# State-space tables of a hybrid backbone on one core: X stored in one transfer, loads for two steps, a second lag buffer, lags read one yield earlier

## Chip, cores and metric

The kernel runs on 1 core of one Trainium2 chip. The metric is device time in microseconds (us) of one execution; the time before is the median of three runs. The core has a matrix engine (TensorE, PE in the profile, with its weight loads as PEld), three elementwise engines (VectorE or DVE, ScalarE or ACT, GpSimd or POOL) and SyncE (SP), which in this kernel issues every transfer to the 16 DMA engines. Everything is float32; the big products are split into three products of a high and a low half.

## What is computed

The reference is a backbone of two layers over 1024 latent tokens and 256 context tokens of width 1024. Layer 0 mixes tokens by differential attention, layer 1 by a bidirectional diagonal complex state-space layer (S5); each mixer is followed by a dense MLP with squared ReLU. The change concerns constants of the S5 layer alone. For each of 2 directions and 64 groups of 16 channels, S5 runs a recurrence over 64 complex states:

```python
lam_bar = jnp.exp(lam * dt)
b_bar = ((lam_bar - 1.0) / lam)[..., None] * b_mat
...
bu = jnp.einsum('gpc,btgc->btgp', b_bar, uc.astype(jnp.complex64))
a_cum, hs = lax.associative_scan(_linear_combine, (a, bu), axis=1)
hs = hs + a_cum * h[:, None]
y = jnp.real(jnp.einsum('gcp,btgp->btgc', c_mat, hs))
```

The kernel doesn't step token by token. It takes 8 tokens at once: powers of lam_bar times b_bar bring 8 tokens' inputs into the states (the matrix X, here transposed from XT), powers of lam_bar times c_mat bring a state to 8 tokens' outputs (W), and within the 8 tokens the inputs reach the outputs through products of both, one small matrix for each distance in time (the lag products, 16 x 16 for each group and lag). All three depend on parameters only, so they are made as tables before the S5 layer runs.

## The kernel before

The program is written with a tile framework: instructions are given in program order, and a scheduler with a model of their times puts each engine's instructions in an order of its own and adds the waits. Every engine, SyncE with its transfers among them, then runs its own list strictly in order, so an instruction that waits holds all behind it on that engine.

**Where the tables are made.** The tables are built beside the down projection of layer 0's MLP, `mlp0_down` (L1596). That stage has 53 blocks. A block runs two of 112 steps q, each of 5 token groups x 3 matmuls (`mm3`, L132 to L134: high x high, high x low, low x high) of 512 columns. For every q, `mlp0_load` (L1572) brings an activation block and a weight block from HBM (transfers U<-Aa, U<-Ta and U<-in_mlp_w) three blocks ahead, and `mlp0_prep` (L1590) splits both into halves: ScalarE copies the high half (L137), VectorE subtracts it from the source (L138). At the end of every run of 16 steps an accumulator is evacuated to the sums FD by ScalarE (L1618) or added to them by VectorE (L1620). After each block's matmuls, `self.step(2)` (L1654) takes two steps of background work, a list of generators; each goes to its next `yield`. The first generator is `s5_phases` (two yields), the second `s5_tables` (L1125). At block 40, what is left of them is drained, and the normalisation of finished token tiles begins (`m0_tile`, L1688): tile 1 loads its residual into `fv(48)` to `fv(52)`.

**The generator `s5_tables`.** It has 32 table steps, in the order `todo`: for each of four groups c, four indices q of direction 0 and four of direction 1; an index covers four (direction, group) positions x. Loop iteration i does, in program order:

- `load(i + 1)` (L1146): three transfers of 64 to 68 KB into slot (i+1) mod 4 of `ins`: the powers tp (from tpd), C (tc, from tcd) and B (tb, from tbd).
- `matrices(i)` (L1151): six VectorE operations, L1153 to L1155 for W and L1160 to L1162 for XT, and one transfer of W to the table `recd`. W and XT have three buffers each.
- a yield, then `products(i - 2)` (L1164): four transposes of XT on TensorE into the PSUM bank `acc` (L1168), one ScalarE copy of the bank to a buffer Xs of 4 x 128 columns (L1169), and two transfers of it to `recd`. There a row has 4 x 192 columns: 128 columns, then the first 64 of them once more. Then four matmuls of tb with W into the bank `acc2` (L1174; the profile counts eight records), one ScalarE copy of their 128 columns to half `q % 2` of the only lag buffer `Ks` (L1176), and after each odd q four transfers of Ks to the table `kd`. Then a yield. Xs has two buffers, `acc` and `acc2` one each.
- after each 8 steps, `lags(c)` (L1182): three transfers bring lag products from kd (kv is a view of it) into k and f0; VectorE adds the two directions' lag 0 (L1188) and the skip term (L1190); one transfer stores k to `ktd`; a yield; four transfers copy ktd with repeated lags to `lagd`; a yield.

The yields of both generators add up to 76, or 38 blocks.

**Where things lie.** U is a tile of 62 KB per partition, of which the tables use `u(0)` to `u(30)` and the projection's loads the part from `u(30)` to `u(61)`. FD (`self.F`, 56 KB) holds the sums in 0 to 40; `s5_phases` works in 40 to 49.5. Offsets count in KB. `recd` and `lagd` are read by the S5 layer (`s5`, L1782), which follows the stage.

Of the kernel before, what the change touches and what calls it, by code (L numbers as in the profile page):

```python
# [9 lines left out]
AF = mybir.ActivationFunctionType  # L10
# [37 lines left out]
def shaped(ap, dims):  # L48
    if len(dims) == 1:
        return ap  # L50
    names = "abcd"[: len(dims)]
    kw = {n: d for n, d in zip(names[1:], dims[1:])}
    return ap.rearrange(f"p ({' '.join(names)}) -> p {' '.join(names)}", **kw)


def bcast(ap, axis, n):
    dims = [list(d) for d in ap.ap]
    dims.insert(axis, [0, n])
    return bass.AP(ap.tensor, ap.offset, dims)
# [11 lines left out]
class Prog:  # L71
# [414 lines left out]
    def lam_setup(self):  # L486
# [5 lines left out]
        st = self.lamc = self.cst.tile([128, 12], F32, name="lamc")  # L492
        nc.vector.tensor_reduce(st[:, 0:2], pr, AX.X, ALU.add)
        nc.scalar.activation(st[:, 2:4], st[:, 0:2], AF.Exp)
# [630 lines left out]
    def s5_tables(self, o, acc, acc2):  # L1125


        nc, I = self.nc, self.I
        v, tt = nc.vector, nc.vector.tensor_tensor
        u = lambda off, *dims: self.view(self.U, off, dims)  # L1130
        ins = [(u(x, 4, 34), u(x + 0.5625, 4, 32), u(x + 1.0625, 4, 32)) for x in (o + 1.5625 * i for i in range(4))]
        Wr = [u(o + 6.25 + 2.25 * i, 4, 9, 16) for i in range(3)]
        t, XTr = u(o + 13, 576), [u(o + 15.25 + 2 * i, 4, 8, 16) for i in range(3)]
        Xr = [u(o + 21.25 + 2 * i, 4, 128) for i in range(2)]
        t4, t2, Ks = shaped(t, (4, 9, 16)), shaped(t[:, 0:512], (4, 8, 16)), u(o + 25.25, 2, 128)
        k, f0, mask, dc = u(o + 26.25, 2, 15, 16), u(o + 28.25, 2, 16), u(o + 28.5, 16), u(o + 28.75, 8)
        self.dma(mask, I["dmask"])
        d0, d1 = u(o + 29, 128)[0:8], u(o + 29.5, 128)[0:8]
        self.dma(d0, I["s5_d"][0].rearrange("(y x) -> y x", x=128))
        v.tensor_copy(d1.rearrange("y (e c j) -> y e j c", c=16, j=4), d0.rearrange("y (e j c) -> y e j c", c=16, j=4))  # L1140
        nc.tensor.transpose(acc[:, 0:8], d1, self.ident[0:8, 0:8])
        nc.scalar.activation(dc, acc[:, 0:8], AF.Copy)
        kv = self.kd.rearrange("d (y e) c j n -> d (e c j) y n", e=2)
        todo = [16 * d + 4 * c + r for c in range(4) for d in range(2) for r in range(4)]

        def load(i):  # L1146
            x0 = 4 * todo[i]
            for dst, src in zip(ins[i % 4], (self.tpd, self.tcd, self.tbd)):
                self.dma(dst, src[:, x0 : x0 + 4])

        def matrices(i):  # L1151
            (tp, tc_, tb_), W, XT, q = ins[i % 4], Wr[i % 3], XTr[i % 3], todo[i]
            tt(W, bcast(tc_[:, :, 0:16], 2, 9), bcast(tp[:, :, 0:9], 3, 16), ALU.mult)  # L1153
            tt(t4, bcast(tc_[:, :, 16:32], 2, 9), bcast(tp[:, :, 9:18], 3, 16), ALU.mult)
            tt(W, W, t4, ALU.add)  # L1155
            d = q // 16
            w0 = 1 - d
            self.dma(shaped(self.recd[q % 16][:, 1536 + 512 * d : 2048 + 512 * d], (4, 128)),
                     W[:, :, w0 : w0 + 8].rearrange("p x i c -> p x (i c)"))
            tt(XT, bcast(tb_[:, :, 0:16], 2, 8), bcast(tp[:, :, 18:26], 3, 16), ALU.mult)  # L1160
            tt(t2, bcast(tb_[:, :, 16:32], 2, 8), bcast(tp[:, :, 26:34], 3, 16), ALU.mult)
            tt(XT, XT, t2, ALU.add)  # L1162

        def products(i):  # L1164
            tb_, W, XT, Xs, q = ins[i % 4][2], Wr[i % 3], XTr[i % 3], Xr[i % 2], todo[i]
            d = q // 16
            for j in range(4):
                nc.tensor.transpose(acc[:, 128 * j : 128 * j + 128], XT[:, j].rearrange("p s c -> p (s c)"), self.ident)  # L1168
            nc.scalar.activation(Xs.rearrange("p x n -> p (x n)"), acc, AF.Copy)  # L1169
            X = shaped(self.recd[q % 16][:, 768 * d : 768 * d + 768], (4, 192))  # L1170
            self.dma(X[:, :, 0:128], Xs)
            self.dma(X[:, :, 128:192], Xs[:, :, 0:64])
            for j in range(4):
                nc.tensor.matmul(acc2[32 * j : 32 * j + 32, 0:128], tb_[:, j],  # L1174
                                 W[:, j, d : d + 8].rearrange("p i c -> p (i c)"), start=True, stop=True)
            nc.scalar.activation(Ks[:, q % 2], acc2[:, 0:128], AF.Copy)  # L1176
            if q % 2:
                for j in range(4):
                    dst = self.kd[d, q % 16 - 1 : q % 16 + 1, :, j].rearrange("h c n -> c h n")
                    self.dma(dst, Ks[32 * j : 32 * j + 16])  # L1180

        def lags(c):  # L1182
            ys = slice(2 * c, 2 * c + 2)
            kk = k.rearrange("p y m c -> p y (m c)")
            self.dma(kk[:, :, 0:128], kv[1][:, ys])
            self.dma(kk[:, :, 128:240], kv[0][:, ys, 16:128])
            self.dma(f0, kv[0][:, ys, 0:16])
            tt(k[:, :, 7], k[:, :, 7], f0, ALU.add)  # L1188
            for y in range(2):
                v.scalar_tensor_tensor(k[:, y, 7], mask, dc[:, 2 * c + y : 2 * c + y + 1], k[:, y, 7], ALU.mult, ALU.add)  # L1190
            self.dma(self.ktd.rearrange("(y e) c j n -> (e c j) y n", e=2)[:, ys], kk)
            yield
            for h in range(4 * c, 4 * c + 4):
                src = self.ktd[h]
                src = bass.AP(src.tensor, src.offset + 16 * 7, [[240, 64], [-16, 8], [1, 128]])
                self.dma(self.lagd[h].rearrange("(s c) (j n) -> (c j) s n", s=8, j=4), src)
            yield

        load(0)
        for i in range(34):  # L1200
            if i < 31:
                load(i + 1)
            if i < 32:
                matrices(i)
            yield
            if i > 1:
                products(i - 2)
                yield
            if i > 1 and (i - 1) % 8 == 0:
                yield from lags((i - 1) // 8 - 1)  # L1210
# [571 lines left out]
    def s5(self):  # L1782
# [54 lines left out]
        def inputs(n, d):  # L1837
            X = slots[n % 2][0] if n else shaped(x_first, (2, 4, 192))
            cols = slice(0, 160) if d == 0 else slice(32, 192)
            for j in range(2):  # L1840
                b = xbank(n, d, j)
                for i in range(4):
                    o = 512 * (i // 2) + 160 * (i % 2)
                    mm(b[:, o : o + 160], X[:, d, i, 64 * j : 64 * j + 128], U[:, 4 * n + i, cols], start=True, stop=True)  # L1844

# [26 lines left out]
        def outputs(n):  # L1872
            X, W1, T, W2, _ = slots[n % 2]
            for i in range(4):
                o = self.bank(6 + n % 2)[:, 128 * i : 128 * i + 128]
                mm(o, U[:, 4 * n + i, 32:160], T[:, i], start=True, stop=False)  # L1876
                for d in range(2):
                    for j, W in enumerate((W1, W2)):
                        mm(o, cs[d][n % 2][j][:, i], W[:, d, i], start=False, stop=d == 1 and j == 1)  # L1879
# [588 lines left out]
```

## Time and profile before

| what | us |
|---|---|
| median of three runs (2878.24 to 2882.3) | 2880.2 |
| the profiled execution | 2870.1 |
| its span, first to last instruction | 2868.3 |
| TensorE busy | 2730.3 |
| VectorE busy | 2016.2 |
| ScalarE busy | 1363.1 |
| GpSimd busy | 1021.6 |
| first load of the tables issued | 1400.7 |
| last lag transfer issued | 1711.8 |

The profile is one execution, on the chip, taken by the hardware profiler. An instruction stands there with its start, its duration, its engine, its line, the tiles it writes and reads (out<-in) and, in brackets, how long its engine had been idle before it and what ended that. "A <- B" in the list of waits reads: A waited for B; then the total, the number of times and the longest. SPq is SyncE's queue of transfers, L80 the helper that issues all of them, so they are told apart by tiles. The granted clock (PEclk) is TensorE's clock as a share of full speed. Busy matmuls overlap: a matmul of 512 columns lasts some 0.39 us, and the next starts before it ends.

### The profile page before, as it was taken

How to read it: one execution, taken by the hardware profiler on the slowest of the kernel's cores; microseconds unless marked ns; L12 is line 12 of the kernel's file. 1: busy time of each engine (PE TensorE's matmuls, PEld its weight loads, DVE VectorE, ACT ScalarE, POOL GpSimd, SP SyncE). 2: the span in 40 equal slices, each digit the busy share in tenths (PEclk: the TensorE clock that was granted, in tenths of full speed). 3: DMA queues.
4: the chain of work that ended last, by engine and by line, in shares of the span. 5: the costliest groups of instructions: out<-in, count | busy, mean ns of one | idle time of the engine just before them, and what ended most of it. 6: DMA issues, size and time to landing. Idle time of an engine off the chain costs nothing. (4 is left out here: it accounts for less than half of the span.)

```text
span 2868.3 us, 43597 instructions
## 1 busy us (share of the span) xinstructions
PE 2730.3 (95%) x15225; PEld 2281.8 (80%) x15225; DVE 2016.2 (70%) x2968; ACT 1363.1 (48%) x2551; POOL 1021.6 (36%) x899
## 2 busy tenths in 40 slices
PE   7999999999899999999999999789999999999999
PEld 4688888888777887878877778688788778878887
DVE  5456788888863666666788767799533597668456
ACT  3425556555554743333444335477444633344443
POOL 2314666676663600000010013588121243336314
PEclk9999999999999999999999999899999999999999
DMA  9955555555826468885899887479743144466544
GB/s 299 309 169 175 153 173 175 177 175 169 255 83 190 120 212 306 296 305 192 272 294 299 260 244 242 156 232 295 253 140 110 59 159 164 158 235 235 165 131 141
DMA packets 447786, 586.33 MB, mean 204 GB/s; under 512 B 60494, under 2 KB 293196, under 8 KB 444364
## 3 DMA queue, kind: packets, MB, share of 16 engines
q1 hardware_dynamic: 447564, 583.53, 63.9%
q8 instruction: 120, 1.97, 0.3%
q14 instruction: 102, 0.84, 0.1%
HBM read 396.38 MB, written 182.82 MB: 202 GB/s over the span
## 5 line engine op out<-in xcount | busy, mean ns | idle before, releaser
L132 PE MATMUL PS<-H 128*128 128x512 f32 x1056 | 416.0, 395 | 8.6 <-DVE FD L1620 5.7
L134 PE MATMUL PS<-H 128*128 128x512 f32 x1056 | 413.8, 393 | 1.6 <-DVE H L2139 1.3
L133 PE MATMUL PS<-H 128*128 128x512 f32 x1056 | 414.8, 393 | 0.0
L132 PE MATMUL PS<-H,R 128*128 128x512 f32 (+1 forms) x828 | 307.5, 374 | 3.6 <-ACT R L137 1.6
L133 PE MATMUL PS<-H,R 128*128 128x512 f32 (+1 forms) x828 | 298.2, 360 | 1.4 <-POOL H L138 1.4
L134 PE MATMUL PS<-H,R 128*128 128x512 f32 (+1 forms) x828 | 297.6, 360 | 0.0
L132 PEld LDWEIGHTS PS<-H 128*128 128x128 f32 x1056 | 199.4, 189 | 55.0 <-issue 6.4
L134 PEld LDWEIGHTS PS<-H 128*128 128x128 f32 x1056 | 199.6, 189 | 45.3 <-DVE H L2139 1.7
L133 PEld LDWEIGHTS PS<-H 128*128 128x128 f32 x1056 | 199.7, 189 | 41.5 <-issue 1.0
L545 ACT ACTIVATE F<-F,stat 128x1280 f32<-128x1280 f32 x128 | 174.4, 1363 | 106.2 <-DVE F L535 105.9
L132 PE MATMUL PS<-R,H 128*128 128x512 f32 x536 | 213.6, 401 | 1.4 <-ACT R L137 1.4
L137 ACT ACTIVATE R<-W 128x512 fp32r<-128x512 f32 (+1 forms) x186 | 130.8, 712 | 172.3 <-PE PS L133 99.2
L133 PE MATMUL PS<-R,H 128*128 128x512 f32 x536 | 210.9, 394 | 0.0
L134 PE MATMUL PS<-R,H 128*128 128x512 f32 x536 | 209.3, 394 | 1.7 <-DVE H L138 1.7
L137 ACT ACTIVATE H<-U 128x640 fp32r<-128x640 f32 x216 | 132.9, 678 | 150.9 <-PE PS L133 104.5
L138 DVE TENSOR_TENSOR H<-W,H 128x512 fp32r<-128x512 f32 (+1 forms) x137 | 124.2, 917 | 103.8 <-ACT H L137 103.1
L138 DVE TENSOR_TENSOR H<-U,H 128x640 fp32r<-128x640 f32 x216 | 165.9, 805 | 39.7 <-ACT H L137 37.8
L535 DVE TENSOR_SCALAR_CACHE_REDUCE F<-PS 128x1280 f32<-128x1280 f32 x128 | 185.2, 1483 | 8.6 <-PE PS L522 8.4
L137 ACT ACTIVATE H<-W 128x512 fp32r<-128x512 f32 (+2 forms) x158 | 96.1, 616 | 191.2 <-PE PS L133 114.3
L132 PEld LDWEIGHTS PS<-H,R 128*128 128x128 f32 x828 | 156.8, 190 | 29.7 <-issue 4.1
L134 PEld LDWEIGHTS PS<-H,R 128*128 128x128 f32 x828 | 156.8, 189 | 25.4 <-issue 0.8
L582 POOL TENSOR_SCALAR R<-F 128x256 fp32r<-128x256 f32 (+1 forms) x128 | 127.1, 993 | 134.3 <-ACT F L581 121.5
(514 smaller groups left out, 6830.0 us busy)
## 6 DMA issues: line engine op xcount, KB each, us to landing
W<-in_mlp_w SPq DMA_DIRECT2D x176, 256.0 KB, 3.0
U<-Aa SPq DMA_DIRECT2D x108, 320.0 KB, 4.5
Aa<-FU SPq DMA_DIRECT2D x91, 320.0 KB, 4.6
Ad<-F SPq DMA_DIRECT2D x112, 256.0 KB, 3.0
W<-Ad SPq DMA_DIRECT2D x112, 256.0 KB, 2.8
FU<-in_mlp_w SPq DMA_DIRECT2D x32, 512.0 KB, 5.5
Ta<-FU SPq DMA_DIRECT2D x16, 1024.0 KB, 3.9
recd<-U SPq DMA_DIRECT2D x64, 256.0 KB, 4.8
```

The costliest lines, as they stand in the source:

```text
L132: mm(out, ah, bh, start=first, stop=False, **kw)
L133: mm(out, ah, bl, start=False, stop=False, **kw)
L134: mm(out, al, bh, start=False, stop=last, **kw)
L137: self.nc.scalar.activation(hi, src, AF.Copy)
L138: (lo_eng or self.nc.vector).tensor_tensor(lo, src, hi.bitcast(F32), ALU.subtract)
L535: ts(p[c], self.PS[:, 1280 * c : 1280 * c + 1280], 1.0, None, ALU.mult, ALU.min, accum_out=sm[:, c : c + 1])
L545: nc.scalar.activation(p[c], p[c], AF.Exp, bias=sm[:, c : c + 1], scale=-1.0, accum_out=sn[:, 0:1] if c else s0[:, u + 1 : u + 2])
L582: nc.gpsimd.tensor_scalar(hi, t, 1.0, 0.0, ALU.mult, ALU.add)
```

## The change

`ins` has three slots of eight positions each in place of four slots of four: one load serves two consecutive steps (the pair p is steps 2p and 2p + 1, which have neighbouring positions), and is issued two steps ahead, on even i. The third slot lies partly in FD. `tables(i)` picks the half of a slot that belongs to step i. Xs has 4 x 192 columns; ScalarE fills 128 of them and, with a second copy, the other 64 from the same bank, and one transfer stores them all. Its second buffer is FD 50 to 53. Ks has two buffers, used in turn by pairs of steps. In `lags` a yield is put between the transfers from kd and VectorE's sums, which makes 80 yields, or 40 blocks. The computation is the same.

```diff
--- before.py
+++ after.py
@@ -1128,11 +1128,12 @@
         nc, I = self.nc, self.I
         v, tt = nc.vector, nc.vector.tensor_tensor
         u = lambda off, *dims: self.view(self.U, off, dims)
-        ins = [(u(x, 4, 34), u(x + 0.5625, 4, 32), u(x + 1.0625, 4, 32)) for x in (o + 1.5625 * i for i in range(4))]
-        Wr = [u(o + 6.25 + 2.25 * i, 4, 9, 16) for i in range(3)]
-        t, XTr = u(o + 13, 576), [u(o + 15.25 + 2 * i, 4, 8, 16) for i in range(3)]
-        Xr = [u(o + 21.25 + 2 * i, 4, 128) for i in range(2)]
-        t4, t2, Ks = shaped(t, (4, 9, 16)), shaped(t[:, 0:512], (4, 8, 16)), u(o + 25.25, 2, 128)
+        ins = [(u(o + 3.0625 * i, 8, 34), u(o + 3.0625 * i + 1.0625, 8, 32), u(o + 3.0625 * i + 2.0625, 8, 32)) for i in range(2)]
+        ins.append((self.fv(53, 8, 34), self.fv(54.0625, 8, 32), u(61, 8, 32)))
+        Wr = [u(o + 6.125 + 2.25 * i, 4, 9, 16) for i in range(3)]
+        t, XTr = u(o + 12.875, 576), [u(o + 15.125 + 2 * i, 4, 8, 16) for i in range(3)]
+        Xr = [u(o + 21.125, 4, 192), self.fv(50, 4, 192)]
+        t4, t2, Ksr = shaped(t, (4, 9, 16)), shaped(t[:, 0:512], (4, 8, 16)), [u(o + 24.125 + i, 2, 128) for i in range(2)]
         k, f0, mask, dc = u(o + 26.25, 2, 15, 16), u(o + 28.25, 2, 16), u(o + 28.5, 16), u(o + 28.75, 8)
         self.dma(mask, I["dmask"])
         d0, d1 = u(o + 29, 128)[0:8], u(o + 29.5, 128)[0:8]
@@ -1143,13 +1144,16 @@
         kv = self.kd.rearrange("d (y e) c j n -> d (e c j) y n", e=2)
         todo = [16 * d + 4 * c + r for c in range(4) for d in range(2) for r in range(4)]
 
-        def load(i):
-            x0 = 4 * todo[i]
-            for dst, src in zip(ins[i % 4], (self.tpd, self.tcd, self.tbd)):
-                self.dma(dst, src[:, x0 : x0 + 4])
+        def load(p):
+            x0 = 4 * todo[2 * p]
+            for dst, src in zip(ins[p % 3], (self.tpd, self.tcd, self.tbd)):
+                self.dma(dst, src[:, x0 : x0 + 8])
+
+        def tables(i):
+            return [t_[:, 4 * (i % 2) : 4 * (i % 2) + 4] for t_ in ins[i // 2 % 3]]
 
         def matrices(i):
-            (tp, tc_, tb_), W, XT, q = ins[i % 4], Wr[i % 3], XTr[i % 3], todo[i]
+            (tp, tc_, tb_), W, XT, q = tables(i), Wr[i % 3], XTr[i % 3], todo[i]
             tt(W, bcast(tc_[:, :, 0:16], 2, 9), bcast(tp[:, :, 0:9], 3, 16), ALU.mult)
             tt(t4, bcast(tc_[:, :, 16:32], 2, 9), bcast(tp[:, :, 9:18], 3, 16), ALU.mult)
             tt(W, W, t4, ALU.add)
@@ -1162,14 +1166,14 @@
             tt(XT, XT, t2, ALU.add)
 
         def products(i):
-            tb_, W, XT, Xs, q = ins[i % 4][2], Wr[i % 3], XTr[i % 3], Xr[i % 2], todo[i]
+            tb_, W, XT, Xs, Ks, q = tables(i)[2], Wr[i % 3], XTr[i % 3], Xr[i % 2], Ksr[i // 2 % 2], todo[i]
             d = q // 16
             for j in range(4):
                 nc.tensor.transpose(acc[:, 128 * j : 128 * j + 128], XT[:, j].rearrange("p s c -> p (s c)"), self.ident)
-            nc.scalar.activation(Xs.rearrange("p x n -> p (x n)"), acc, AF.Copy)
-            X = shaped(self.recd[q % 16][:, 768 * d : 768 * d + 768], (4, 192))
-            self.dma(X[:, :, 0:128], Xs)
-            self.dma(X[:, :, 128:192], Xs[:, :, 0:64])
+            rows = shaped(acc, (4, 128))
+            nc.scalar.activation(Xs[:, :, 0:128], rows, AF.Copy)
+            nc.scalar.activation(Xs[:, :, 128:192], rows[:, :, 0:64], AF.Copy)
+            self.dma(self.recd[q % 16][:, 768 * d : 768 * d + 768], Xs.rearrange("p x n -> p (x n)"))
             for j in range(4):
                 nc.tensor.matmul(acc2[32 * j : 32 * j + 32, 0:128], tb_[:, j],
                                  W[:, j, d : d + 8].rearrange("p i c -> p (i c)"), start=True, stop=True)
@@ -1185,6 +1189,7 @@
             self.dma(kk[:, :, 0:128], kv[1][:, ys])
             self.dma(kk[:, :, 128:240], kv[0][:, ys, 16:128])
             self.dma(f0, kv[0][:, ys, 0:16])
+            yield
             tt(k[:, :, 7], k[:, :, 7], f0, ALU.add)
             for y in range(2):
                 v.scalar_tensor_tensor(k[:, y, 7], mask, dc[:, 2 * c + y : 2 * c + y + 1], k[:, y, 7], ALU.mult, ALU.add)
@@ -1198,8 +1203,8 @@
 
         load(0)
         for i in range(34):
-            if i < 31:
-                load(i + 1)
+            if i < 30 and i % 2 == 0:
+                load(i // 2 + 1)
             if i < 32:
                 matrices(i)
             yield
```

## The prediction

> **What bounds the kernel now.** I read the page first, then the busy times of the stretch in which the edited functions run, then the waits there, then single waits in the order of time.
>
> ```profile
> PE 2730.3 (95%) x15225; PEld 2281.8 (80%) x15225; DVE 2016.2 (70%) x2968; ACT 1363.1 (48%) x2551; POOL 1021.6 (36%) x899
> ```
>
> TensorE is busy for 95% of the span, so the rest of the kernel pays only where TensorE stands still. The busy times by stretch (length, busy time and instructions of each engine, granted clock, DMA share, GB/s) show how the tables' stage, 1400 to 1720 us, stands:
>
> ```profile
> 1400.00:1560.00 160.00, 155.14 (x807) 120.78 (x806) 138.84 (x203) 70.20 (x130) 16.10 (x17) 1.00 0.98 298
> 1560.00:1720.00 160.00, 153.39 (x770) 122.23 (x771) 116.70 (x178) 61.88 (x119) 6.91 (x4) 0.97 0.86 258
> 1587.20:1590.50 3.30, 3.30 (x9) 2.56 (x8) 2.26 (x4) 3.30 (x7) 0.00 (x0) 0.50 0.99 235
> 1653.20:1658.60 5.40, 5.26 (x12) 4.12 (x13) 5.40 (x10) 0.28 (x1) 0.00 (x0) 0.50 0.96 295
> 1620.00:1623.30 3.30, 3.30 (x17) 2.70 (x15) 3.27 (x6) 0.54 (x2) 0.00 (x0) 1.00 1.01 313
> ```
>
> TensorE lacks 4.86 and 6.61 us of the two halves, 11.47 us together. DMA is nearly full (0.98 and 0.86), VectorE has 255.5 us of 320. In two short stretches the granted clock is 0.50 (9 matmuls in 3.30 us, where 17 fit at 1.00). These two follow the two longest of TensorE's pauses; its own rows with idle time in front of them, in order of time, are all here:
>
> ```profile
> 1442.25 0.63 PE L1168 MATMUL PS<-ident,U 128*128 128x128 f32 x4 [1.64 <-ACT H L137]
> 1502.20 0.43 PE L1174 MATMUL PS<-U 128*32 128x128 f32 x8 [1.01 <-ACT U L1176]
> 1518.61 0.42 PE L1174 MATMUL PS<-U 128*32 128x128 f32 x8 [1.25 <-ACT U L1176]
> 1534.69 0.43 PE L1174 MATMUL PS<-U 128*32 128x128 f32 x8 [0.28 <-ACT U L1176]
> 1550.51 0.43 PE L1174 MATMUL PS<-U 128*32 128x128 f32 x8 [0.68 <-ACT U L1176]
> 1585.68 0.43 PE L1174 MATMUL PS<-U 128*32 128x128 f32 x8 [2.63 <-ACT U L1176]
> 1653.34 0.79 PE L132 MATMUL PS<-H 128*128 128x512 f32 x1 [3.91 <-DVE FD L1620]
> ```
>
> Their sum is 11.40 us. Half the clock over 3.30 + 5.40 us costs half of it, 4.35 us. So 15.75 us is all that these tables make the matmuls wait: the most that a change of their buffers and transfers can bring in this stage. Who makes whom wait (total, times, longest):
>
> ```profile
> ACT U L1176 <- DMA kd<-U: 51.1, 12, 8.5
> DVE U L1160 <- DMA U<-tbd: 26.4, 13, 7.9
> ACT U L1169 <- DMA recd<-U: 19.8, 6, 5.6
> DVE U L1188 <- DMA U<-kd: 8.2, 3, 4.3
> ACT H L137 <- PE PS L133: 86.7, 24, 5.2
> SPq L80 <- DMA ktd<-U: 11.7, 3, 6.6
> ```
>
> **Two lag buffers.** L1176 copies a lag product into Ks and waits until the store of the pair before has left it: 12 waits, 51.1 us. While it waits, acc2 stays full, and L1174 stops TensorE's queue: five of the seven pauses, 1.01 + 1.25 + 0.28 + 0.68 + 2.63 = 5.85 us, and the clock after the last one, 3.30 / 2 = 1.65 us. With a second buffer the copy waits for the store of two pairs back, two steps further away. A step is about 8 us (transposes L1168 at 1632.83, 1640.65 and 1648.48 below), so two steps give 16 us, and the longest of the waits is 8.5. All twelve should go: **7.5 us**.
>
> **Loads for two steps.** The 3.91 us pause is this chain:
>
> ```profile
> 1632.83 0.60 PE L1168 MATMUL PS<-ident,U 128*128 128x128 f32 x4
> 1634.34 0.38 SPq L80 DMA_DIRECT2D ktd<-U  x1
> 1640.65 0.60 PE L1168 MATMUL PS<-ident,U 128*128 128x128 f32 x4
> 1641.42 2.56 SPq L80 DMA_DIRECT2D lagd<-ktd  x4
> 1645.30 1.17 SPq L80 DMA_DIRECT2D U<-tbd  x1
> 1648.48 0.60 PE L1168 MATMUL PS<-ident,U 128*128 128x128 f32 x4
> 1649.39 0.69 DVE L1160 TENSOR_TENSOR U<-U 128x512 f32<-128x512 f32 x1 [7.86 <-DMA U<-tbd]
> 1652.61 0.68 DVE L1620 TENSOR_TENSOR FD<-FD,PS 128x512 f32<-128x512 f32 x1
> ```
>
> SyncE stores ktd and its next instruction, the lag read, waits for that store to land; the tb load stands behind it and is issued 11 us after ktd. VectorE waits 7.86 us at L1160, and the evacuation L1620, queued behind, holds the accumulator. Before, the load of step i+1 takes the slot of step i-3, whose products run in step i-1, and VectorE wants it from about step i: one step, 8 us, of cover. After, a pair's load is issued two steps before the pair's first matrices, and the products that free its slot ran a step before that: two steps, 16 us. The 7.86 us fits into what is added. So 3.91 us and the clock behind it, 5.40 / 2 = 2.70 us, go: **6.6 us**. SyncE's own wait on ktd (11.7 us in three) I leave where it is.
>
> On the clock the Trainium skill speaks too ("TensorE: Matmul & The Clock Gate", table of practical rules): no pause over about 3 us between bursts of matmuls, else the clock halves. By that rule only the 3.91 us pause would be followed by half clock, and the gain would be 1.65 us less. The trace disagrees: the pause of 2.63 us has its half-clock stretch too, so I keep both.
>
> **X in one store.** Removed are 32 transfers, added 32 copies on ScalarE:
>
> ```profile
> L1169 ACT ACTIVATE U<-PS 128x512 f32<-128x512 f32 x32 | 18.9, 589 | 24.2 <-DMA recd<-U 19.8 <-PE PS L1168 4.4
> L1176 ACT ACTIVATE U<-PS 128x128 f32<-128x128 f32 x32 | 8.7, 273 | 53.8 <-DMA kd<-U 51.1 <-PE PS L1174 2.6
> L80 SPq DMA_DIRECT2D recd<-U x96: 359/385/2052, 1416.5 to 1696.8; - x96
> q1 hardware_dynamic: 106787, 88.71, 91.3%
> q1 hardware_dynamic: 18482, 34.62, 65.3%
> ```
>
> A copy of 128x256 lies between 273 and 589 ns; on the line through both it is 378 ns, 12.1 us in all. ScalarE has 132 us of 320 busy and waits 86.7 us for TensorE (24 times, "ACT H L137 <- PE PS L133"), so it runs ahead of what TensorE needs. I cost the copy at nothing; without that cover it would be at most 12.1 us. It keeps acc 0.38 us longer, of the 7.8 us until the next transposes.
>
> The two queue rows are q1's packets, MB and share of 16 DMA engines, over 1400 to 1720 us and over 1240 to 1390 us (larger packets). That is 4675 and 1567 engine-us; solved for two prices they give 11.1 ns a packet and 39.3 us a MB. X had 2 x 512 packets a step (512 and 256 bytes), after 128 of 3072 bytes if a row isn't cut: 28,700 fewer in all; the loads halve theirs, 6,100 fewer. About 34,800 x 11.1 ns / 16 = 24 us of 292 that each DMA engine is busy: estimated share 0.91 to about 0.84, or no change if rows are cut. SyncE issues 32 + 48 fewer DMAs, 80 x 0.385 = 31 us. None of this is on the path by itself; it lets what stands in the queue land earlier. I count nothing.
>
> The X buffers stay two. Their 19.8 us of waits end in one pause, the first (1.64 us): ScalarE stood 5.63 us for the store, the halves came late to VectorE, and its L1162 ended at 1442.10, just before the transposes. X leaves in one transfer now, but only after both copies. Ends: all of it gone or none; I keep it, **0**, since the buffers' number is the same.
>
> **Lags ahead.** L1188 waits 8.2 us in three; four yields are added, so the steps grow from 76 to 80, two for each of the 40 blocks before the tables must be done. Two of the four lag groups (the second and the fourth) get a whole block between read and sum; in the other two both steps fall in one block, and the yield moves the lag read behind ktd's store into the next block instead. No pause names L1188: **0**. The table work ends one to two blocks later, before the 40th block still; X's second buffer now lies where tile 1 of the next stage loads its residual, so that load, early today, moves to the tables' end. Its tile has the 100 us to the end of the stage: 0.
>
> **Sum.** 7.5 + 6.6 = 14.1 us. DMA stays above 0.8 and the order of issue is drawn anew, so small pauses can come up elsewhere. The trace doesn't show them; ends are 0 and what all small pauses of today come to (1.64 + 1.01 + 1.25 + 0.28 + 0.68 = 4.86 us). I take two of the mean size 0.97, 1.9 us, nearer to the low end because the waits behind them lose their cause. Forecast: **12.2 us less**. The profiled execution would go from 2870.1 to 2857.9 us. The shown median, 2880.2, is 10.1 us (0.35%) above the profiled execution; I carry the difference over: **2868.0**.
>
> **Rivals.**
> *Half of it.* SyncE's blocked stretch at ktd stays, and the pair's loads land late again; only the lag part is gained, 7.5 us: 2872.7. For it: the ktd wait is untouched. Against it: 16 us of cover against a wait of 7.86. Chance 0.10.
> *The wait changes its name.* Products now stop at L1169 for X instead of L1176 for Ks: same place in ScalarE's queue, same accumulators, one store that starts later. What is won at Ks is lost at X, within 5.8 us of before: 2880. For it: DMA is at 0.98 early on and recd has 19.8 us of waits already. Against it: 26 of 32 steps don't wait for recd. Chance 0.16.
> *Slower: X's two buffers become the rhythm.* If the single store, behind its second copy and behind SyncE's other issues, lands later than the two steps until its buffer is wanted, every step pays what the first pause paid, 1.64 us of TensorE for 5.63 us of ScalarE. It decides against the change from 14.1 / 1.64 = 9 steps; at 15 of the 32 steps it is 24.6 - 14.1 = 10.5 us slower, 2891; at all 32, 38 us slower. Against it: fewer packets and issues, and a landing of 4.6 us median (longest 5.5) for the two stores now. Chance 0.12.
>
> ```profile
> DMA to landing us min/median/max: 2.3/4.6/5.5
> ```
>
> *The forecast's case*, 8 to 16 us less: 0.62.
>
> **How the numbers follow.** What a measurement of this kernel can tell from no change is about 0.2%, 5.8 us. Faster: 0.62 + 0.10 = 0.72; within: 0.16; slower: 0.12. The low end is all 15.75 us gone and some 2 us more from a freer queue, 2862. The high end takes in the half case and nearly all of the renamed wait, 2884; left out are the slower rival and a sliver on each side.
>
> **What would show it.** Right: no row "ACT U L1176 <- DMA kd<-U" of more than 1 us, L1160 without a wait of 5 us, TensorE at over 158 us in each of the two halves, a granted clock of 1.00 throughout, the last matmul of the tables' stage and of the kernel about 12 us earlier. Wrong: L1169 waiting for recd in more than nine steps; a half-clock stretch between 1400 and 1720; DMA share still 0.98; or a stage that ends 12 us earlier and a total that doesn't follow, in which case the next stage has kept a bound of its own.

## The result, and the profile after

The changed kernel takes 2858.93 us (median of 6 runs, 2854.94 to 2861.59) where the kernel before took 2878.94 us (6 runs, 2873.83 to 2882.3). The ratio is 0.9934, 95% interval 0.9917 to 0.9952: about 19 us less, 14 to 24 by the interval. The prediction had the sign, but 2868.0 is 9.1 us too high, and the measured time lies below its range. The profiled execution went from 2870.1 to 2854.94 us, 15.2 less where 12.2 were forecast.

The page of the changed kernel, its span and the engines' busy times. Inserted lines shift the numbers from here on: L1168, L1169, L1174 and L1176 of before are L1172, L1174 (with the second copy, L1175), L1178 and L1180; L1160, L1188 and L1620 are L1164, L1193 and L1625.

```profile
span 2853.1 us, 43450 instructions
...
PE 2727.6 (96%) x15225; PEld 2282.9 (80%) x15225; DVE 2020.9 (71%) x2968; ACT 1369.6 (48%) x2583; POOL 1024.8 (36%) x899
```

TensorE has as much to do as before, in 15.2 us less. Busy times by stretch (length, then busy time and instructions of PE, PEld, DVE, ACT and POOL, granted clock, DMA share, GB/s):

```profile
1400.00:1560.00 160.00, 159.76 (x823) 126.54 (x822) 145.46 (x214) 76.91 (x151) 18.87 (x17) 1.00 0.98 323
1560.00:1720.00 160.00, 160.00 (x828) 128.17 (x827) 125.31 (x180) 74.65 (x150) 16.64 (x14) 1.00 0.83 257
1720.00:1800.00 80.00, 79.19 (x350) 65.30 (x349) 57.38 (x72) 34.34 (x64) 25.71 (x24) 1.00 0.64 196
```

In the tables' stage TensorE lacked 11.47 us of 320 and lacks 0.24 now; the clock is 1.00 in both halves. Of TensorE's rows with a pause in front, one is left in the stage, and one of 0.81 us behind it, where the rows are normalised (1.82 us before):

```profile
1464.16 0.63 PE L1172 MATMUL PS<-ident,U 128*128 128x128 f32 x4 [0.23 <-DVE U L1166]
...
1756.90 0.47 PE L132 MATMUL PS<-H 128*128 128x512 f32 x1 [0.81 <-DVE FD L1625]
```

Who waits for whom in the stage (total, times, longest):

```profile
ACT H L137 <- PE PS L133: 132.1, 31, 4.9
...
DVE U L1193 <- DMA U<-kd: 4.3, 4, 1.9
...
ACT U L1174 <- DMA recd<-U: 3.4, 1, 3.4
```

The waits of 51.1 us for kd and 26.4 us for tbd have no row any more. recd, which waited 19.8 us with the same two buffers, waits 3.4. ScalarE now waits mostly for TensorE, which is what an engine with time to spare should do. q1's packets fell, its share of the DMA engines hardly did (before 106787 and 91.3%):

```profile
q1 hardware_dynamic: 72345, 92.48, 89.7%
```

By instructions that stand in both traces, the changed kernel is 2.6 us late when the tables begin (the program is the same up to there), 15.1 us early at the end of the stage and 14.7 us early at the last mark. So this pair of executions gained 17.7 us in the stage (16.5 of them by 1720 us, where the prediction gave 15.75 as the most), and the rest of the kernel carries it to the end.

### The profile page after: what moved, and what is told of

It is laid out like the page before. It is cut to its first block, busy times and chain, and to the rows that moved or that the text cites. A ratio compares the mean times of both kernels' runs of the same rounds, so it can differ in the third digit from the quotient of the medians.

```text
span 2853.1 us, 43450 instructions
## 1 busy us (share of the span) xinstructions
PE 2727.6 (96%) x15225; PEld 2282.9 (80%) x15225; DVE 2020.9 (71%) x2968; ACT 1369.6 (48%) x2583; POOL 1024.8 (36%) x899
## 5 line engine op out<-in xcount | busy, mean ns | idle before, releaser
L137 ACT ACTIVATE H<-U 128x640 fp32r<-128x640 f32 x216 | 131.9, 674 | 174.6 <-PE PS L133 145.8
L137 ACT ACTIVATE R<-W 128x512 fp32r<-128x512 f32 (+1 forms) x186 | 130.7, 711 | 172.3 <-PE PS L133 98.1
L137 ACT ACTIVATE H<-W 128x512 fp32r<-128x512 f32 (+2 forms) x158 | 95.7, 613 | 187.8 <-PE PS L133 113.7
```

The source lines that it names most:

```text
L137: self.nc.scalar.activation(hi, src, AF.Copy)
```

## The experiments

Two recd buffers that stopped waiting pointed away from buffers. **The theory:** all four waits (kd, tbd, recd, U<-kd) are one thing, SyncE's list of transfers running late. SyncE issues in order; in 1400 to 1700 us it issued 458 transfers before, 207 us of issuing, and much of the rest went into waits inside the list. The changed kernel issues 386. The kd store of one pair is an example. Kernel before, single instructions (start, length): L1176 makes the odd step's product, and SyncE issues the last of its four stores 13 us later; the next pair's copy waits 8.54 us for it, and TensorE pauses 2.63 us.

```profile
1568.88 0.26 ACT L1176 ACTIVATE U<-PS 128x128 f32<-128x128 f32 x1
...
1580.92 1.86 SPq L80 DMA_DIRECT2D kd<-U  x4
...
1585.35 0.28 ACT L1176 ACTIVATE U<-PS 128x128 f32<-128x128 f32 x1 [8.54 <-DMA kd<-U]
```

The changed kernel, the same at another pair: the stores start 0.4 us after the product.

```profile
1550.54 0.27 ACT L1180 ACTIVATE U<-PS 128x128 f32<-128x128 f32 x1
1551.21 1.98 SPq L80 DMA_DIRECT2D kd<-U  x4
```

I call the time from the end of that copy to the end of the fourth issue the **lag of kd**: median over the 16 pairs 11.0 us before and 2.9 us after. **Rival A** is the prediction: each part takes away the wait that it names. **Rival B:** fewer packets free the DMA engines. Each kernel below ran in five rounds against the kernel before on the same chip.

| kernel | edit | time / before | ratio, 95% | lag of kd | SyncE issues | TensorE lacks |
|---|---|---|---|---|---|---|
| e1 | before, two lag buffers | 2872.99 / 2876.42 | 0.9992 (0.9982 to 1.0002) | 13.2 | 454 | 14.50 |
| e2 | before, pair loads | 2856.84 / 2876.42 | 0.9937 (0.9924 to 0.9951) | 6.4 | 428 | 0.00 |
| e3 | before, X in one store | 2863.25 / 2876.42 | 0.9965 (0.9952 to 0.9979) | 7.8 | 435 | 2.69 |
| e4 | before, yield in the lags | 2873.02 / 2876.42 | 0.9984 (0.9971 to 0.9997) | 9.1 | 459 | 5.85 |
| e5 | before, single loads two steps ahead | 2869.98 / 2875.48 | 0.9979 (0.9967 to 0.9991) | 8.8 | 459 | 10.32 |
| e6 | e3, store cut in two | 2874.2 / 2875.48 | 0.9997 (0.9984 to 1.0009) | 10.1 | 451 | 11.64 |
| e7 | e2, 48 tiny transfers more | 2870.42 / 2875.48 | 0.9988 (0.9970 to 1.0007) | 10.0 | 462 | 8.53 |
| l2 | after, old loads | 2870.7 / 2875.48 | 0.9980 (0.9963 to 0.9997) | 7.6 | 428 | 2.49 |
| e13 | after, 32 tiny transfers more | 2860.86 / 2876.08 | 0.9950 (0.9929 to 0.9972) | 8.7 | 416 | 0.86 |
| e9 | after, 80 tiny transfers more | 2869.3 / 2876.21 | 0.9981 (0.9967 to 0.9995) | 10.8 | 455 | 8.94 |
| e8 | before, X stored by ScalarE | 2875.19 / 2876.21 | 1.0000 (0.9989 to 1.0011) | 4.4 | 395 | 10.33 |
| e10 | after, X and kd stored by ScalarE | 2875.79 / 2876.21 | 1.0001 (0.9988 to 1.0015) | 4.9 | 282 | 8.14 |
| e11 | before, X stored by GpSimd | 2887.67 / 2876.08 | 1.0039 (1.0021 to 1.0057) | 3.2 | 383 | 24.99 |
| e12 | before, kd stored by GpSimd | 2859.34 / 2876.08 | 0.9936 (0.9914 to 0.9958) | 2.3 | 407 | 0.79 |
| f2 | after, kd stored by GpSimd | 2865.36 / 2876.65 | 0.9968 (0.9955 to 0.9981) | 2.3 | 324 | 0.43 |

The times are medians, in us. The last three columns are worked out from each kernel's trace, so from one execution each: the slowest of twelve for e9, the fastest for e3, e8 and the changed kernel. "TensorE lacks" is what its busy time misses of the 320 us from 1400 to 1720, 11.47 before and 0.24 in the changed kernel.

As long as SyncE stores X, this lack goes with the number of its issues: at most 2.69 us with 324 to 435 of them, 5.85 us and more with 451 to 462. The three kernels in which another engine stores X (e8, e10, e11) don't fit, and are taken up below.

### One part alone

**e1: the second lag buffer**

```diff
-        t4, t2, Ks = ..., u(o + 25.25, 2, 128)
+        t4, t2, Ksr = ..., [u(o + 25.25, 2, 128), u(61, 2, 128)]
...
+        Ks = Ksr[i // 2 % 2]
```

> Before, with the second lag buffer alone. Theory (each pause of TensorE goes with the wait that made it, and the parts add): the waits of L1176 for the kd store go, and with them five pauses of 5.85 us and 1.65 us of half clock: 7.5 us less, ratio 0.9974; the waits for tb stay. Rival (the transfers carry it: fewer packets let everything land earlier): the packets are those of before, so within 2 us of before.

The median is 3.4 us lower, the ratio's interval takes in 1; 7.5 us were forecast for this part. The kd row is gone, as forecast. The waits of e1, and a pause of TensorE:

```profile
ACT U L1169 <- DMA recd<-U: 41.2, 13, 7.7
...
DVE U L1160 <- DMA U<-tbd: 26.5, 10, 7.5
...
DVE U L1188 <- DMA U<-kd: 12.9, 3, 8.2
```

```profile
1653.53 0.80 PE L132 MATMUL PS<-H 128*128 128x512 f32 x1 [12.68 <-DVE FD L1620]
```

ScalarE waits at L1169 for X instead (19.8 us before, 41.2 now), and behind the tbd wait stands a single pause of 12.68 us. The wait changed its name: the prediction's second rival, which holds for this part alone.

**e2: the loads for two steps**, three slots of eight positions, as in the change:

```diff
...
-            if i < 31:
-                load(i + 1)
+            if i < 30 and i % 2 == 0:
+                load(i // 2 + 1)
```

> Before, with the loads for two steps alone. Theory: the waits of L1160 for tb go, and with them one pause of 3.91 us and 2.70 us of half clock: 6.6 us less, ratio 0.9977; the waits of L1176 for kd stay. Rival (transfers): 6,100 of the 34,800 packets go, so about a sixth of the 20 us, 3.5 us less, and both kinds of wait get a little shorter.

This part alone gives 18 us (0.0063 x 2876), as much as all four together, and it is the part that was forecast at 6.6. Busy times of e2 by stretch, and two of its waits:

```profile
1400.00:1560.00 160.00, 160.00 (x831) 125.53 (x829) 145.26 (x213) 73.61 (x135) 16.64 (x17) 1.00 1.01 324
1560.00:1720.00 160.00, 160.00 (x822) 128.43 (x819) 124.69 (x182) 69.89 (x133) 15.05 (x10) 1.00 0.89 263
```

```profile
ACT U L1180 <- DMA kd<-U: 20.4, 10, 5.9
...
DVE U L1164 <- DMA U<-tbd: 0.6, 1, 0.6
```

TensorE has no pause left in the stage, with one lag buffer. The ten waits for kd are still there, but shorter (longest 5.9 us for 8.5), and none reaches TensorE. So the five pauses at L1174 were no want of a buffer.

**e3: X in one store**, with two buffers of 4 x 192, was forecast at 0:

```diff
...
+            nc.scalar.activation(Xs[:, :, 0:128], rows, AF.Copy)
+            nc.scalar.activation(Xs[:, :, 128:192], rows[:, :, 0:64], AF.Copy)
+            self.dma(self.recd[q % 16][:, 768 * d : 768 * d + 768], Xs...)
```

> Before, with X stored in one transfer alone. Theory: at most the first pause goes, 0 to 1.6 us less; the waits for kd and tb stay. Rival (transfers): 28,700 of the 34,800 packets go, so most of the gain is here: 12 us less or more, with the waits for kd and tb gone without a buffer of their own.

It gives 10 us (0.0035 x 2876). Its waits still have a kd and a tbd row, both smaller than before:

```profile
ACT U L1176 <- DMA kd<-U: 35.4, 10, 8.2
...
DVE U L1160 <- DMA U<-tbd: 17.1, 8, 4.8
```

**e4: the yield in the lags**

```diff
             self.dma(f0, kv[0][:, ys, 0:16])
+            yield
```

> Before, with the yield in the lags alone. Theory: no pause names L1188, 0 us, ratio 1.000. Rival (the blocked stretch of SyncE between the ktd store and the lag read is what made tb and kd late, and the yield moves it apart): the 3.91 us pause with its half clock goes, 5 us less or more.

5 us by the ratio (interval 1 to 8), where 0 was forecast. kd still waits 42.4 us, and TensorE pauses 3.81, 2.04 and, in the section behind the stage, 5.11 us. The 3.91 us pause of the kernel before is gone, as the rival has it. No transfer is taken away; SyncE's list is drawn in another order.

### Cover, packets or issues?

**e5: only the cover of e2.** Six slots of four positions, each step's loads issued two steps ahead, the transfers as many as before:

```diff
...
+        load(1)
...
-            if i < 31:
-                load(i + 1)
+            if i < 30:
+                load(i + 2)
```

> Before, with single loads issued two steps ahead into six slots: the cover of the pair loads, with the 96 issues and the packets of before. Theory of cover (VectorE never waits for tb, so the halves and all that SyncE holds for them come on time): as with pair loads, about 18 us less, L1160 without waits for tb. Theory of SyncE's issues (its list runs late because it is long): 96 issues stay, under 5 us less. Theory of packets: 0.

6 us of e2's 18. The tbd wait is gone, by the two steps of cover, and with it the pause for which it was blamed; but kd still waits 40.7 us (51.1 before), and TensorE stops for it. A wait of e5, and a pause:

```profile
ACT U L1180 <- DMA kd<-U: 40.7, 11, 9.0
```

```profile
1588.08 0.66 PE L1178 MATMUL PS<-U 128*32 128x128 f32 x8 [4.05 <-ACT U L1180]
```

**e6: only the packets of e3.** The same long rows of X, but in two transfers of 64 partitions, so that SyncE issues as many as before:

```diff
-            self.dma(self.recd[q % 16][:, ...], Xs...)
+            for h in range(2):
+                p = slice(64 * h, 64 * h + 64)
+                self.dma(self.recd[q % 16][p, ...], Xs[p]...)
```

> Before, with X of 192 columns stored in two transfers of 64 partitions: the 28,700 packets fewer of the one store, with the 64 issues of before. Theory of packets: as with one store, 10 us less, ratio 0.9965. Theory of SyncE's issues: the issues are those of before, so under 4 us less. Theory of cover: the loads are those of before, so what X in one store gained must come from its own wait for recd; 0 to 4 us.

Nothing is left of e3's 10 us: the interval is 0.9984 to 1.0009. The packets did fall: q1 has 78053 from 1400 to 1720 us, as e3 has (78857), where the kernel before has 106787. So rival B falls here. The waits of e6 are longer than e3's again:

```profile
ACT U L1178 <- DMA kd<-U: 45.2, 9, 9.6
DVE U L1160 <- DMA U<-tbd: 29.1, 11, 7.7
```

**e7: e2 with 48 near-empty transfers**, 64 bytes each into a corner of FD that nobody reads, three in each odd step, which gives SyncE back the issues that pair loads save:

```diff
...
+            for _ in range(3 if i < 32 and i % 2 else 0):
+                self.dma(extra.next(), I["dmask"][0:1])
```

> Pair loads alone, with 48 transfers of 64 bytes put back into SyncE's list, three on every odd step; they go to a place that nobody reads. The computation is the same. Theory of SyncE's issues: 48 x 0.38 us are back, and with them the waits for tb or kd and 10 us or more of the 18. Theories of cover and of packets: no change from pair loads alone, 18 us below before.

3 us are left of 18 (interval -2 to 9), with e2's slots and cover, and its packets but for the 48. Its waits:

```profile
ACT U L1180 <- DMA kd<-U: 53.6, 10, 8.7
...
PE PS L1178 <- ACT U L1180: 8.5, 4, 3.9
```

The wait for kd is back as it was before (51.1 us). This is the most direct evidence: 48 x 64 bytes are no load for the DMA engines (q1's share is 91.7%, in e2 94.3%), but they stand in SyncE's list, at 0.25 us each.

### The other way round

**l2: the changed kernel with the old loads**

```diff
...
-            if i < 30 and i % 2 == 0:
-                load(i // 2 + 1)
+            if i < 31:
+                load(i + 1)
```

> The changed kernel with the loads of before (one step each, four slots, one step ahead). Theory of cover: waits of L1165 for tb come back, with a pause or two; at most what X in one store gained stays, 6 to 10 us below before. Theory of issues or packets: 32 issues and 28,700 packets fewer stay, 10 us below before or more, since a second lag buffer helps too, without waits for tb.

Without pair loads 6 us of the 19 are left, less than e3 has alone. In l2's profile, of an execution 7 us faster than its median, two pauses remain, 2.49 us at the first step and this one behind the stage:

```profile
1760.49 0.77 PE L132 MATMUL PS<-H 128*128 128x512 f32 x1 [5.54 <-DVE FD L1622]
```

In the tables' stage l2 lacks no more than e3; in this execution the rest of its loss lies behind the stage. Why it lies there is not settled.

**e13 and e9: the changed kernel with 32 and 80 tiny transfers**

```diff
+            if i < 32:                                       # e13
+                self.dma(extra.next(), I["dmask"][0:1])
...
+            for _ in range((2, 3)[i % 2] if i < 32 else 0):   # e9
+                self.dma(extra.next(), I["dmask"][0:1])
```

> The changed kernel with 32 transfers of 64 bytes in SyncE's list, one a step, to a place that nobody reads. Theory of SyncE's list: the loss grows with the number; 80 cost 14 us, 32 cost 3 to 8 us, kd stores 4 to 7 us after their product. Rival (these small transfers do harm in another way, by the order that is drawn anew, say): the loss is as large as with 80, or nil.

> The changed kernel with 80 transfers of 64 bytes put back into SyncE's list, five on every two steps, to a place that nobody reads; the computation is the same. Theory of SyncE's list: the 80 issues that the change took away are back, the kd stores are issued late again (6 us or more), and at least a third of the 20 us is lost; not all, since Ks and the loads have more cover. Rivals (cover, buffers, packets): they are those of the changed kernel, so no loss, ratio 0.993 to 0.994.

Of the 19 us, 32 transfers leave 14 (0.0050 x 2876) and 80 leave 5. The lag of kd goes from 2.9 to 8.7 and 10.8 us. For 32 transfers the lag came out above the 4 to 7 us expected, the cost of 5 us within its range. The lag alone doesn't set the time: at 8.7 us e13 lacks 0.86 us of TensorE, at 8.8 us e5, which has one lag buffer, lacks 10.32. In e9 the lateness shows at another name (waits up to 1800 us):

```profile
DVE U L1193 <- DMA U<-kd: 29.7, 4, 12.1
...
PE PS L132 <- DVE FD L1628: 9.6, 2, 5.2
```

### The issues on another engine's list

**e12: the 64 kd stores, of the kernel before, issued by GpSimd.** Nothing else is changed:

```diff
-                    self.dma(dst, Ks[32 * j : 32 * j + 16])
+                    nc.gpsimd.dma_start(out=dst, in_=Ks[32 * j : 32 * j + 16])
```

> Before, with the 64 kd stores of 16 KB each issued by GpSimd. Theory of SyncE's list: 64 issues less of almost no bytes, the waits for tb and recd get short, the wait for kd goes, 10 to 18 us less. Rival: the wait for kd goes and nothing else moves, as with a second lag buffer, 2 us less.

18 us (0.0064 x 2876), the whole gain, with one lag buffer, old loads and two X stores. The waits of e12, and its transfers of kd (ns shortest, median, longest):

```profile
DVE U L1160 <- DMA U<-tbd: 14.5, 9, 3.3
ACT U L1169 <- DMA recd<-U: 12.1, 4, 4.5
...
ACT U L1176 <- DMA kd<-U: 1.9, 1, 1.9
```

```profile
L1180 POOL DMA_DIRECT2D kd<-U x64: 507/507/738, 1431.4 to 1688.3; - x64
```

GpSimd has nothing else to issue here, so the stores start at once (lag 2.3 us), and what stays on SyncE's list moves up: tbd waits 14.5 us for 26.4.

**e8 and e10: ScalarE issues** X of the kernel before, and X and kd of the changed one:

```diff
-            self.dma(X[:, :, 0:128], Xs)
+            nc.scalar.dma_start(out=X[:, :, 0:128], in_=Xs)
...
```

> Before, with the two X stores of each step issued by ScalarE in place of SyncE: 64 issues leave SyncE's list; transfers, packets, buffers and covers are those of before. Theory (SyncE's list is full and runs late, and every store and load behind it lands late): the kd stores are issued 3 to 7 us after their product in place of 11 us, the pauses mostly go, 10 to 18 us less. Rivals (cover of the loads; packets; the number of lag buffers): none of these is touched, 0 to 3 us.

> The changed kernel with the X stores and the kd stores issued by ScalarE: 96 more issues leave SyncE's list. Theory of SyncE's list: the tables' stage of the changed kernel has under 0.5 us of pauses left, so nothing is left to win there, 0 to 2 us below the changed kernel, ratio 0.992 to 0.994; the kd stores are issued within 2 us. Rival (ScalarE's issues hold its copies, which the matmuls need): slower than the changed kernel by 3 us or more.

Both are at 1.000 of before, so e8 gains nothing and e10 loses all that the changed kernel had won. The theory's numbers missed, though SyncE's list is shorter (395 and 282) and kd is early (4.4 and 4.9 us). ScalarE's own queue pays, as the rival of e10 has it. e10, single instructions, and its transfers of kd:

```profile
1511.93 2.87 ACTq L1184 DMA_DIRECT2D kd<-U  x4
...
1516.12 2.41 ACT L137 ACTIVATE H<-U 128x640 fp32r<-128x640 f32 x4 [4.49 <-DMA kd<-U]
```

```profile
L1184 ACTq DMA_DIRECT2D kd<-U x64: 309/326/1008, 1430.8 to 1707.5; - x64
```

The copy L137, which rounds the tiles that the matmuls read, starts after 4.49 us in which ScalarE computes nothing and issues four transfers; such waits of L137 for kd are 46.5 us in e10. In e8 its waits for the X stores are 20.2 us.

**e11: GpSimd issues X of the kernel before**, the same edit with nc.gpsimd:

```diff
-            self.dma(X[:, :, 0:128], Xs)
+            nc.gpsimd.dma_start(out=X[:, :, 0:128], in_=Xs)
...
```

> Before, with the two X stores of each step issued by GpSimd, which stands idle in most of the stage: 64 issues leave SyncE's list and no copy that the matmuls need stands behind them. Theory of SyncE's list: kd stores 3 to 7 us after their product, pauses mostly gone, 8 to 18 us less. Rival (it isn't SyncE's list; with ScalarE as issuer nothing was gained either): 0 to 3 us less though the kd stores come early.

11 us slower (0.0039 x 2876): a miss. The waits of e11, GpSimd's own and ScalarE's:

```profile
POOL recd L1172 <- issue: 126.0, 31, 6.3
POOL recd L1171 <- issue: 86.0, 22, 6.1
ACT U L1169 <- DMA recd<-U: 101.4, 22, 9.7
```

The kd stores followed each other at once on GpSimd; these do not. It stands up to 6.3 us before an X store that waits for nothing the trace shows, 212 us of idle time in all. Its list became the late one, and X's two buffers the rhythm: the prediction's slower rival, brought about by hand.

**f2: both gains together,** the changed kernel with e12's edit, an attempt at a better one:

```diff
-                    self.dma(dst, Ks[32 * j : 32 * j + 16])
+                    nc.gpsimd.dma_start(out=dst, in_=Ks[32 * j : 32 * j + 16])
```

> The changed kernel with the 64 kd stores issued by GpSimd: the two ways of making SyncE's list shorter together, 144 issues fewer than before. Theory: each of them alone takes TensorE's pauses out of the tables' stage, and there is nothing more to win there: within 2 us of the changed kernel, ratio 0.992 to 0.994. Rival (the gains add): 0.987.

9 us less than before (0.0032 x 2876), 10 worse than the changed kernel. TensorE is busy for 319.57 us of 320 in the stage, and pauses behind it:

```profile
1720.00:1800.00 80.00, 72.97 (x314) 59.96 (x313) 57.22 (x68) 33.41 (x62) 21.59 (x20) 0.96 0.72 216
```

```profile
1765.66 0.77 PE L132 MATMUL PS<-H 128*128 128x512 f32 x1 [7.03 <-DVE FD L1625]
```

Once the stage is full there is nothing more to win in it. The pause at the normalisation differs from kernel to kernel: none in e3 and e7, 0.5 us in e12, 0.81 in the changed kernel, 5.54 in l2, 7.03 in f2. What sets it was not tried; every edit redraws the order of the lists, and this is the part of the differences that stays open. Since a new order can be worth some 10 us (f2 against the changed kernel), no single kernel here settles the cause. That edits of three kinds (fewer issues in e2 and e3, issues put back in e6, e7 and e9, issues moved in e12) all go the way of the count does. No kernel here beats the changed one; e12 equals it with one line.

## Why the prediction was too small, point by point

**Where the time is lost: right.** The stage 1400 to 1720 us, the pauses of TensorE and their clock. All marks named as "right" came: no kd row, no tbd wait, over 158 us of TensorE in each half, clock 1.00, and an earlier end (15 us for 12). Of the marks named as "wrong" one came too, the DMA share of 0.98 in the first half: the freer DMA engines of the prediction's estimate are not there. The sign and the place held; the causes of the parts didn't. That 12.2 us came near the 15.2 of the profiled execution is partly luck: the parts shared out the pauses of that one trace, and whatever removes the pauses brings their sum.

**"None of this is on the path by itself ... I count nothing": the step that failed.** It said this of the 80 issues fewer, which were priced at 0 and carry most of the change. With 48 issues put back e2 loses 15 of 18 us, with 80 put back the changed kernel loses 14 of 19, and with 64 taken elsewhere (e12) the kernel before gains 18. Its other half, fewer packets, was rightly counted at nothing (e6).

**"Two lag buffers", 7.5 us: wrong cause.** Alone it gives at most 5 us by e1's interval, and the wait is renamed: it was long because the store was issued 11 us late. What the second buffer adds beside the other parts was not tried; that it lets the list run late without harm, as in e13, is argued, not shown.

**"Loads for two steps", 6.6 us: right wait, wrong size.** The cover does what was worked out (e5: no tbd wait, 6 us). The other 12 us need the 48 issues fewer: with as many put back (e7), 3 us are left in all.

**X "0, since the buffers' number is the same": wrong.** e3 gives 10 us, by 32 issues fewer; the 1.64 us pause that was kept is gone in the changed kernel. The extra copies cost nothing that shows: ScalarE waits 132.1 us for TensorE.

**Lags ahead, 0:** e4 measured 5 us (1 to 8); it takes no transfer away, so the new order of the lists is the likely cause, which was not tried apart.

**The sum.** In e1 to e4 the parts gain 0.0008 + 0.0063 + 0.0035 + 0.0016 = 0.0122, together 0.0066: they remove the same lateness, so they don't add.

**The allowance of 1.9 us for new pauses** was not wanted in the stage: 0.24 us are left.

**The carried difference.** Of the 9.1 us that the forecast is too high, 3.0 lie in the profiled execution (2857.9 against 2854.94), and 6.1 in the step "I carry the difference over": 10.1 us from profile to median before, 4.0 after (2858.93 - 2854.94). The pauses differ from execution to execution: the kernel before took 2865.7 to 2888.0 us in 34 runs on one chip, e2, without pauses in the stage, 2854.9 to 2860.1 in 5. This suggests that the profiled execution of before was a light one, and that the others had more to lose than its 15.75 us; none of the others was profiled.

**The rivals.** The half case fell with the forecast. The renamed wait is e1, the slower one e11; neither is the whole change, since both need a list that stays late.

**The clock rule** of the Trainium skill ("TensorE: Matmul & The Clock Gate", Why this matters for your kernels, the table there: no pause over about 3 us) was rightly set aside for the 2.63 us pause. Below 3 us it is no rule either way in these traces (see the end).

## What to carry to other kernels

When several waits for DMAs sit on one stage, first see how late the issuing engine's list runs: take the time from the instruction that makes the data to the issue of its store, and if it is long, count issues before buffers. A second buffer for a store that is issued late passes the wait on to the next transfer of the list; fewer issues remove it, and so can an idle engine's list for a few small stores (kd on GpSimd did, X on GpSimd or ScalarE did not). Parts with a common cause are priced together, and a profile of one execution isn't the median where pauses differ from run to run.

## What the runs showed of the hardware

- **Which list.** The Trainium skill says that issuing from several engines saves only the sequencer's time for the issue, "which is usually small relative to the DMA itself" ("DMA: Bandwidth & Descriptors", Issuing engines are not separate DMA queues). Here that saving is the whole gain with GpSimd and kd (0.9936), nothing with ScalarE and X (1.0000), and a loss with GpSimd and X (1.0039).
- **GpSimd.** Issuing a kd store took 507 ns at the median, with the next right behind; before X stores it stood 212 us idle in 53 waits, 4 us each. Why was not tried.
- **Clock.** Of TensorE's pauses from 1400 to 1800 us in all these traces, none under 2.0 us had a stretch of granted clock 0.50 with it, six of ten between 2.0 and 3.0 us had (2.04 in e4, 2.63 before; not 2.21 in e2 nor 2.94 in e11), and all from 3.3 us on; e10's 3.23 us lay inside a stretch that an earlier pause had begun. The stretches are mostly 3.41 or 6.83 us long, and some begin within the pause: with e1's 12.68 us it was 13.65, of which 5.49 came after the pause.
- **Packets.** A third fewer packets in q1 (106787 to 72345) changed its share from 91.3% to 89.7%, not to the 84% worked out from two prices.
